# Expert stage: scatter products and transposes in two groups a slot, both conditional branches between the down products, no zero fill

## The chip, the cores and the metric

The kernel runs on one core of a Trainium2 chip. The metric is the device time of one execution in microseconds; of the kernel before there are three timed runs, and their median stands for it. All times below are in microseconds unless marked ns. TensorE's granted clock is either full (1.00, 2.4 GHz) or half (0.50, 1.2 GHz).

## The reference

Two network blocks over 512 tokens of width 1024, in float32. The change lies in the feed-forward part of the first block, a mixture of 32 experts in four groups; each token goes to the best two experts of its best group:

```python
g_sel = top_k(softmax(ht @ router_group), 1)
top_vals, top_idx = top_k(expert logits of that group, 2)
top_w = softmax(top_vals) * p_group
for every expert e:
    act = silu(ht @ w_gate[e]) * (ht @ w_up[e]) * combine[:, e]      # 1024 -> 256
    y = y + act @ w_down[e]                                          # 256 -> 1024
```

The result is scaled by a gain and added to the residual stream. The rest (a mixer with two kinds of recurrent heads ahead of it, and two attention and convolution blocks behind it) is not touched.

## The kernel before

**Slots.** The stage (`moe`, called from `moe_block`) goes through 16 slots. A slot serves two experts, x and x + 16, whose tokens share one tile of 128 rows: normally 64 rows each, and up to 32 more for one of the two where the other has few. The rows of a slot are gathered by an indirect DMA on POOL's queue into one of three buffers (`gather`, tile xg), scaled on ScalarE, and transposed on TensorE (`moe_xt`: tile pxt in PSUM, then xt by VectorE).

**Steps of a slot.** `moe_up` multiplies the transposed rows with gate and up weights (tile gu). Each expert uses only its half of the array's columns: one matmul for 64 columns into pgA, one for the other 64 into pgB, eight steps k of the contraction; two such products run side by side. A float32 product stands in the trace as two records, so one k is two pairs of records. If one of the two experts has more than 64 rows, a conditional branch adds products on 32 columns (`narrow`); else a zero fill writes those rows of the banks. `moe_act` is the activation step: ScalarE takes Silu of the gate half into tile sa or sb, VectorE multiplies by the token weight and the up half; there are four pieces, two for sa, two for sb. `moe_st` transposes sa and sb (tile pst, copied to st). `moe_down` multiplies with the down weights (tile dn) into two banks py, again on half columns, with a second conditional branch in the middle (`narrow` rows). ScalarE copies py to yh, rounded, and VectorE makes the rest yl. `moe_hot` makes a one-hot matrix toh of token numbers on VectorE. `moe_back` multiplies yh and yl with toh on the full array (tile pb), eight scatter groups of two products, and VectorE adds each into the residual stream xT.

**Order.** Each engine does its instructions in the order in which the program writes them; there is no planner in this stage. Slots overlap by that order: in iteration x the products of slot x run over k = 0 to 7; behind k = 1 come the transposes pst of slot x - 1; behind k = 1 to 6 one scatter group each of slot x - 2, and two behind k = 7. Then come the conditional products of slot x, its activation step, the transposes pxt and the gather for slot x + 1, the scaling for x + 2, and the down products of slot x - 1. In iterations 0 and 1 the routing of overflow tokens is done in between (`route_extra`, `route_extra2`). `pump` issues the weight loads on SP's queue at the end of an iteration, into rings of six gu and eight dn tiles.

**PSUM.** Tag c has four banks in rotation for pxt, pst, pb and py. Three banks of tag d and one of tag a hold pgA and pgB of two slots.

**Helpers.** All matmuls are recorded at L199 (`mm`), transposes at L202 (`tr`), ScalarE's work at L196, VectorE's at L205, L210, L214.

Of the kernel before, what the change touches and what calls it, by code (L numbers as in the profile page):

```python
# [10 lines left out]
F32 = mybir.dt.float32  # L11
# [10 lines left out]
P = 128  # L22
T = 512
D = 1024
KD = 8
# [150 lines left out]
class Build:  # L176
# [1686 lines left out]
        self.nc.vector.tensor_copy(st[:, 0:2 * n], pt[:, 0:2 * n * P].rearrange("p (k t) -> p k t", t=P))  # L1863
        return st

    def moe_down(self, mp, st, dn, wide, narrow=(), need=None):


        pys = [self.pc("py") for _ in dn]

        def part(k, parts, start, stop):
            for py, d in zip(pys, dn):
                for i, r, n in parts:
                    self.mm(py[r:r + n], st[:, 2 * i + k, r:r + n], d[i][:, k, :], start, stop)
        part(0, wide, True, False)
        if narrow:
            with self.tc.If(need > 0):
                for k in range(2):
                    part(k, narrow, False, False)
        part(1, wide, False, True)  # L1880
        ys = []
        for py in pys:
            yh, yl = [mp.tile([P, T], F32R, tag="y", bufs=4, name=n) for n in ("yh", "yl")]
            self.act(yh, py, AF.Copy)
            self.tt(yl, py, yh.bitcast(F32), OP.subtract)
            ys.append((yh, yl))
        return ys
# [67 lines left out]
    def moe(self, mp, pump, tab_d):  # L1955

        tab, ids = self.tab, self.ids
        n = NMAIN
        rows = ((slice(0, 64), slice(64, 96)), (slice(32, 64), slice(64, 128))), ((slice(0, 32), slice(64, 128)), (slice(0, 64), slice(96, 128)))

        parts = ((((0, 0, 64), (1, 64, 64)), ((0, 64, 32), (1, 32, 32))), (((1, 0, 64), (0, 64, 64)), ((0, 0, 32), (1, 96, 32))))
        g, xt, ps, s, st, y, oh, need = {}, {}, {}, {}, {}, {}, {}, {}

        def scale(x):
            if x < n:
                self.act(g[x], g[x], AF.Copy, scale=tab[:, 3, x:x + 1])

        def start(x):
            if x == 0:
                scale(x)  # L1970
            xt[x] = self.moe_xt(mp, g.pop(x))
            if x + 3 < n:
                g[x + 3] = self.gather(ids[:, x + 3:x + 4], x + 3)
            need[x] = self.nc.tensor.value_load(self.need[0:1, x:x + 1])
            ps[x] = [self.pd("pgA"), self.pd("pgB") if x % 2 == 0 else self.ps.tile([P, T], F32, tag="a", bufs=self.ps_a, name="pgB")]

        def narrow(x):

            with self.tc.If(need[x] > 0) as c:
                for k in range(KD):  # L1980
                    self.moe_up(ps[x], xt[x], gus, k, parts[x % 2][1])
            with c.Else():
                for i, r, m in parts[x % 2][1]:
                    self.mm(ps[x][i][r:r + m, :], self.zero[:, 0:m], self.zero)

        for x in range(3):
            g[x] = self.gather(ids[:, x:x + 1], x)
        pump(0, 0, eng="gpsimd")
        start(0)
        scale(1)  # L1990
        for x in range(n + 2):
            gus = [self.gus[x + 16 * i] for i in range(2)] if x < n else None
            for k in range(KD):
                if x < n:
                    self.moe_up(ps[x], xt[x], gus, k, parts[x % 2][0])
                if k == 1 and 0 < x <= n:
                    st[x - 1] = self.moe_st(mp, s.pop(x - 1))
                for j in ((), range(k - 1, k), range(6, KD))[min(k, 1) + k // 7] if x > 1 else ():
                    self.moe_back(y[x - 2][j // 4], oh[x - 2], j // 4, (j % 4,))
            if x < n:  # L2000
                narrow(x)
                i = x % 2
                s[x] = self.sA[i], self.sB[i]
                for e in range(2):
                    for r in rows[i][e]:
                        self.moe_act(s[x][e], ps[x][e], tab[:, 1 + e, x:x + 1], r)
                del ps[x], xt[x]
            if x + 1 < n:
                start(x + 1)
            if x + 2 < n:  # L2010
                scale(x + 2)
            if x == 0:
                self.route_extra([mp.tile([P, T], F32, tag="y", bufs=4, name="xs") for _ in range(4)])
            if x == 1:
                self.route_extra2()
                self.dma("scalar", tab_d, tab)
            if 0 < x <= n:
                c = x - 1
                y[c] = self.moe_down(mp, st.pop(c), [[self.dns[c + 16 * e, h] for e in range(2)] for h in range(2)],
                                     *parts[c % 2], need[c])  # L2020
                oh[c] = self.moe_hot(tab[:, 0, c:c + 1])
            pump(2 * (x + 1), 4 * x)

    def moe_extra(self, mp, mw, wg, wu, wd, tab_d, gu_bufs, dn_bufs):
# [763 lines left out]
```

## Time and profile before

| | |
|---|---|
| median of 3 runs | 2766.24 (2765.49 to 2769.7) |
| profiled execution | 2763.61, its span 2761.9 |
| TensorE busy | 2524.8 (91%) |
| VectorE busy | 1546.4 (56%) |
| ScalarE busy | 936.0 (34%) |
| POOL busy | 961.5 (35%) |
| mean DMA rate | 152 GB/s |

How to read it: a row of a timeline has the start, the duration, engine and line, the operation, output and inputs, and in square brackets the time for which the engine stood idle before it and who released it. Matmul records overlap, as the engine is pipelined: the distance between starts tells the rate, and the duration of one record is longer. The expert slots lie between 793 and 1133.

### The profile page before, as it was taken

The page shows a single profiled execution, that of the slowest core. Times are in us where ns is not written, and L with a number is a line of the kernel's source. Part 1 is how long each engine was busy: PE and PEld are TensorE (multiplying, and loading weights), DVE is VectorE, ACT ScalarE, POOL GpSimd, SP SyncE. Part 2 cuts the span into 40 slices and gives each one's busy share as a digit, 9 for nine tenths or more (in the row PEclk, how much of TensorE's full clock was granted, in tenths as well). Part 3 has the DMA queues.
Part 4 walks back from the last instruction along what each step waited for, and adds up shares of the span by engine and source line. Part 5 has one row for each costly group of instructions (what it writes and reads, how often), then busy time and mean ns, then how long its engine had stood idle before and what let it go on. Part 6 is the DMA issues. An engine that isn't in the chain of part 4 may idle for free.

```text
span 2761.9 us, 35101 instructions
## 1 busy us (share of the span) xinstructions
PE 2524.8 (91%) x13640; PEld 1839.8 (67%) x13640; DVE 1546.4 (56%) x2483; ACT 936.0 (34%) x1536; POOL 961.5 (35%) x649
## 2 busy tenths in 40 slices
PE   7777888787969999889999999999999999999999
PEld 4576776565633333556777777878766777888887
DVE  4996595454255655555455388885444345453523
ACT  3424223443221111233344332323332344442422
POOL 1444454422320000243563333434332343344443
PEclk8889998779979999899999999999999999999999
DMA  9356565643289984333455345553231325132321
GB/s 265 99 159 183 157 181 179 194 128 126 95 318 349 344 311 174 107 107 103 139 165 169 107 140 171 193 171 116 74 109 51 95 75 193 62 106 92 107 89 64
DMA packets 336316, 419.06 MB, mean 152 GB/s; under 512 B 37752, under 2 KB 279904, under 8 KB 327824
## 3 DMA queue, kind: packets, MB, share of 16 engines
q1 hardware_dynamic: 317008, 378.13, 42.1%
q10 hardware_dynamic: 14480, 24.23, 2.6%
q0 software_dynamic: 4656, 14.35, 1.6%
q8 instruction: 114, 1.87, 0.3%
q14 instruction: 58, 0.48, 0.1%
HBM read 387.64 MB, written 33.21 MB: 152 GB/s over the span
## 4 chain that ended last, share of the span: by engine, by line
PE 44%; DVE 6%; issue 3%; POOL 2%; ACT 2%; DMA 2%; ACTq 0%; POOLq 0%; DVEq 0%
PE pd L199 35%; DVE adacc L214 2%; PE psc L199 2%; POOL wlo L205 2%; PE tm L199 2%; PE ptot L199 1%; DMA raw<-in_w_up 1%; DVE cv L214 1%; PE pc L199 1%; PE po L199 1%; DVE h L214 1%; PE pz L199 1%; PE pso L199 1%; PE pst L199 1%; PE prr L199 1%
## 5 line engine op out<-in xcount | busy, mean ns | idle before, releaser
L205 POOL TENSOR_TENSOR wlo<-raw,whi 128x1024 fp32r<-128x1024 f32 (+3 forms) x317 | 721.6, 2283 | 1219.2 <-ACT whi L196 1068.1
L199 PE MATMUL pd<-h,whi 128*128 128x512 f32 (+1 forms) x3440 | 1096.0, 401 | 31.7 <-DVE stg L214 6.7
L199 PEld LDWEIGHTS pd<-h,whi 128*128 128x128 f32 x3440 | 646.3, 193 | 188.3 <-issue 28.6
L199 PE MATMUL pd<-h,wlo 128*128 128x512 f32 (+1 forms) x1720 | 673.8, 392 | 21.2 <-POOL wlo L205 21.2
L196 ACT ACTIVATE whi<-raw 128x1024 fp32r<-128x1024 f32 (+3 forms) x319 | 314.0, 994 | 264.4 <-PE pd L199 127.5
L199 PEld LDWEIGHTS pd<-h,wlo 128*128 128x128 f32 x1720 | 330.9, 192 | 93.5 <-POOL wlo L205 25.5
L214 DVE SCALAR_TENSOR_TENSOR adacc<-raw,cs,adacc 128x256 f32<-128x256 f32 x288 | 211.0, 733 | 9.4
L199 PE MATMUL pd<-fyh,whi 128*128 128x512 f32 (+1 forms) x546 | 205.4, 376 | 8.6 <-ACT whi L196 5.2
L214 DVE SCALAR_TENSOR_TENSOR cv<-pd,vec,cv 128x511 f32<-128x511 f32 (+1 forms) x176 | 131.8, 749 | 143.4 <-ACT cv L196 137.9
L199 PE MATMUL pd<-fyh,wlo 128*128 128x512 f32 (+1 forms) x546 | 202.0, 370 | 5.0 <-POOL wlo L205 5.0
L199 PE MATMUL pd<-fyl,whi 128*128 128x512 f32 (+1 forms) x546 | 202.1, 370 | 2.8 <-DVE fyl L205 2.8
L199 PE MATMUL pgB<-gu,xt 128*64 128x512 f32 (+1 forms) x304 | 153.7, 613 | 3.0 <-DVE xt L205 3.0
L199 PE MATMUL pgA<-gu,xt 128*64 128x512 f32 (+1 forms) x304 | 153.7, 613 | 0.0
L214 DVE SCALAR_TENSOR_TENSOR xTl<-pd,mod,xTl 128x512 f32<-128x512 f32 (+1 forms) x73 | 49.4, 683 | 186.1 <-PE pd L199 186.1
L199 PE MATMUL tm<-whi,h 128*128 128x256 f32 x640 | 129.3, 295 | 8.3 <-ACT whi L196 8.0
L214 DVE SCALAR_TENSOR_TENSOR xT<-pb,mod,xT 128x512 f32<-128x512 f32 x128 | 93.6, 748 | 77.2 <-PE pb L199 77.1
L199 PEld LDWEIGHTS pd<-fyh,whi 128*128 128x128 f32 x546 | 105.1, 192 | 39.8 <-ACT whi L196 8.9
L199 PEld LDWEIGHTS pd<-fyh,wlo 128*128 128x128 f32 x546 | 104.9, 192 | 24.3 <-POOL wlo L205 7.3
L199 PEld LDWEIGHTS pd<-fyl,whi 128*128 128x128 f32 x546 | 105.1, 192 | 19.6 <-DVE fyl L205 3.6
L199 PEld LDWEIGHTS tm<-whi,h 128*128 128x128 f32 x640 | 106.2, 199 | 9.6 <-ACT whi L196 8.3
L199 PE MATMUL tm<-wlo,h 128*128 128x256 f32 x320 | 93.3, 292 | 7.7 <-POOL wlo L205 7.6
L196 ACT ACTIVATE cv<-pd,vec 128x512 f32<-128x512 f32 x88 | 68.2, 776 | 94.6 <-PE pd L199 94.0
(563 smaller groups left out, 3404.5 us busy)
## 6 DMA issues: line engine op xcount, KB each, us to landing
raw<-in_ada SPq DMA_DIRECT2D x64, 1024.0 KB, 5.6
raw<-in_w_in SPq DMA_DIRECT2D x54, 1024.0 KB, 5.4
raw<-in_w_up SPq DMA_DIRECT2D x44, 1024.0 KB, 5.0
gu<-in_wg SPq DMA_DIRECT2D x30, 1024.0 KB, 4.8
gu<-in_wu SPq DMA_DIRECT2D x30, 1024.0 KB
dn<-in_wd SPq DMA_DIRECT2D x59, 512.0 KB, 4.7
raw<-in_w_dn SPq DMA_DIRECT2D x16, 1024.0 KB, 5.2
raw<-in_wo SPq DMA_DIRECT2D x12, 1024.0 KB, 5.2
```

The source lines that it names most:

```text
L196: return self.nc.scalar.activation(out, in_, func, **kw)
L199: return self.nc.tensor.matmul(out, lhsT, rhs, start=start, stop=stop)
L205: return (eng or self.nc.vector).tensor_tensor(out, a, b, op=op)
L214: return (eng or self.nc.vector).scalar_tensor_tensor(out, a, s, b, op0=op0, op1=op1)
```

## The change

`narrow` keeps only its taken branch; the zero fill of the rows that a slot doesn't use is done once for each of the two pairs of banks ahead of the first slot, and the banks are held in a list `banks` and not allocated anew. The transposes of the gathered rows, the gather, the load of the branch flag (`rows_of`) and the scaling move from the end of the iteration to k = 4 of the products before. The eight scatter groups come in fours behind k = 1 and k = 4. `moe_down` gets an argument `between`, and calls the conditional up products of the current slot between its first and second half; the activation step comes behind `moe_down` and `moe_hot`.

```diff
-    def moe_down(self, mp, st, dn, wide, narrow=(), need=None):
+    def moe_down(self, mp, st, dn, wide, narrow=(), need=None, between=None):
...
         part(0, wide, True, False)
+        if between is not None:
+            between()
         if narrow:
...
-        def start(x):
-            if x == 0:
-                scale(x)
+        def rows_of(x):
             xt[x] = self.moe_xt(mp, g.pop(x))
             if x + 3 < n:
                 g[x + 3] = self.gather(ids[:, x + 3:x + 4], x + 3)
             need[x] = self.nc.tensor.value_load(self.need[0:1, x:x + 1])
-            ps[x] = [self.pd("pgA"), self.pd("pgB") if x % 2 == 0 else self.ps.tile([P, T], F32, tag="a", bufs=self.ps_a, name="pgB")]
 
         def narrow(x):
 
-            with self.tc.If(need[x] > 0) as c:
+            with self.tc.If(need[x] > 0):
                 for k in range(KD):
                     self.moe_up(ps[x], xt[x], gus, k, parts[x % 2][1])
-            with c.Else():
-                for i, r, m in parts[x % 2][1]:
-                    self.mm(ps[x][i][r:r + m, :], self.zero[:, 0:m], self.zero)
...
-        start(0)
+
+        banks = [[self.pd("pgA"), self.pd("pgB")], [self.pd("pgA"), self.ps.tile([P, T], F32, tag="a", bufs=self.ps_a, name="pgB")]]
+        for x in range(2):
+            for i, r, m in parts[x][1]:
+                self.mm(banks[x][i][r:r + m, :], self.zero[:, 0:m], self.zero)
+        scale(0)
+        rows_of(0)
         scale(1)
         for x in range(n + 2):
             gus = [self.gus[x + 16 * i] for i in range(2)] if x < n else None
+            if x < n:
+                ps[x] = banks[x % 2]
+
             for k in range(KD):
                 if x < n:
                     self.moe_up(ps[x], xt[x], gus, k, parts[x % 2][0])
                 if k == 1 and 0 < x <= n:
                     st[x - 1] = self.moe_st(mp, s.pop(x - 1))
-                for j in ((), range(k - 1, k), range(6, KD))[min(k, 1) + k // 7] if x > 1 else ():
-                    self.moe_back(y[x - 2][j // 4], oh[x - 2], j // 4, (j % 4,))
+                if k == 4 and x + 1 < n:
+                    rows_of(x + 1)
+                    scale(x + 2)
+                    if x == 1:
+                        self.route_extra2()
+                        self.dma("scalar", tab_d, tab)
+                if k in (1, 4) and x > 1:
+                    self.moe_back(y[x - 2][k // 4], oh[x - 2], k // 4, range(4))
+            if 0 < x <= n:
+                c = x - 1
+                y[c] = self.moe_down(mp, st.pop(c), [[self.dns[c + 16 * e, h] for e in range(2)] for h in range(2)],
+                                     *parts[c % 2], need[c], (lambda: narrow(x)) if x < n else None)
+                oh[c] = self.moe_hot(tab[:, 0, c:c + 1])
+            elif x == 0:
+                narrow(0)
             if x < n:
-                narrow(x)
                 i = x % 2
                 s[x] = self.sA[i], self.sB[i]
                 for e in range(2):
                     for r in rows[i][e]:
                         self.moe_act(s[x][e], ps[x][e], tab[:, 1 + e, x:x + 1], r)
                 del ps[x], xt[x]
-            if x + 1 < n:
-                start(x + 1)
-            if x + 2 < n:
-                scale(x + 2)
             if x == 0:
                 self.route_extra([mp.tile([P, T], F32, tag="y", bufs=4, name="xs") for _ in range(4)])
-            if x == 1:
-                self.route_extra2()
-                self.dma("scalar", tab_d, tab)
-            if 0 < x <= n:
-                c = x - 1
-                y[c] = self.moe_down(mp, st.pop(c), [[self.dns[c + 16 * e, h] for e in range(2)] for h in range(2)],
-                                     *parts[c % 2], need[c])
-                oh[c] = self.moe_hot(tab[:, 0, c:c + 1])
             pump(2 * (x + 1), 4 * x)
```

On VectorE, from the transposed rows of one slot to the copy of pst, the order before was as follows (sa and sb are the tiles of the activation step, yl and toh belong to the down products of the slot before).

```order
L214 SCALAR_TENSOR_TENSOR sa_6321<-sa_6321,tab,pgA 32x256
L214 SCALAR_TENSOR_TENSOR sa_6321<-sa_6321,tab,pgA 64x256
L214 SCALAR_TENSOR_TENSOR sb_6323<-sb_6323,tab,pgB 64x256
L1877 UNCONDITIONAL_BRANCH
L214 SCALAR_TENSOR_TENSOR sb_6323<-sb_6323,tab,pgB 32x256
L205 TENSOR_TENSOR xt<-pxt,b_5891 128x512 x2
L205 TENSOR_TENSOR yl<-py,yh 128x512 x2
L210 TENSOR_SCALAR toh<-tokens,tab 128x512
L1863 COPY st<-pst 128x512
```

After the change the same stretch of VectorE stands so:

```order
L205 TENSOR_TENSOR xt<-pxt,b_5891 128x512 x2
L214 SCALAR_TENSOR_TENSOR xT<-pb,mod_81,xT 128x512 x4
L1978 UNCONDITIONAL_BRANCH
L1879 UNCONDITIONAL_BRANCH
L205 TENSOR_TENSOR yl<-py,yh 128x512 x2
L210 TENSOR_SCALAR toh<-tokens,tab 128x512
L214 SCALAR_TENSOR_TENSOR sa_6321<-sa_6321,tab,pgA 32x256
L214 SCALAR_TENSOR_TENSOR sa_6321<-sa_6321,tab,pgA 64x256
L214 SCALAR_TENSOR_TENSOR sb_6323<-sb_6323,tab,pgB 64x256
L214 SCALAR_TENSOR_TENSOR sb_6323<-sb_6323,tab,pgB 32x256
L1863 COPY st<-pst 128x512
```

The four products of the activation step have moved from ahead of xt and yl to behind yl and toh, directly ahead of the copy of pst.

On ScalarE the end of one iteration before:

```order
L1979 UNCONDITIONAL_BRANCH
L196 ACTIVATE sa_6321<-pgA 32x256
L196 ACTIVATE sa_6321<-pgA 64x256
L196 ACTIVATE sb_6323<-pgB 64x256
L196 ACTIVATE sb_6323<-pgB 32x256
L1877 UNCONDITIONAL_BRANCH
L196 ACTIVATE xg_6315<-xg_6315,tab 128x1024
L196 ACTIVATE yh<-py 128x512 x2
```

And after the change:

```order
L196 ACTIVATE xg_6315<-xg_6315,tab 128x1024
L1978 UNCONDITIONAL_BRANCH
L1879 UNCONDITIONAL_BRANCH
L196 ACTIVATE yh<-py 128x512 x2
L196 ACTIVATE sa_6321<-pgA 32x256
L196 ACTIVATE sa_6321<-pgA 64x256
L196 ACTIVATE sb_6323<-pgB 64x256
L196 ACTIVATE sb_6323<-pgB 32x256
```

The two copies yh, which read the down products, stood behind the four Silus and stand ahead of them now; the scaling of xg has moved to the front.

On TensorE the stretch around the gathered rows' transposes pxt, before:

```order
L199 MATMUL pgB<-zero 32x512
L1979 UNCONDITIONAL_BRANCH
L202 MATMUL pxt<-const_ident,xg_6315 128x128 x8
L1974 TENSOR_LOAD need
L199 MATMUL py<-dn,st 64x512 x4
```

And after:

```order
L199 MATMUL pgA<-gu,xt 64x512
L202 MATMUL pxt<-const_ident,xg_6315 128x128 x8
L1974 TENSOR_LOAD need
L199 MATMUL pb<-toh,yh 128x512
L199 MATMUL pb<-toh,yl 128x512
```

The zero fill ahead of pxt is gone, and pxt is followed by scatter products and not by the down products py.

## Rows read from the trace of the kernel before

**Rows 1.** Part 1 of the page: busy time, share of the span, instructions.

```profile
PE 2524.8 (91%) x13640; PEld 1839.8 (67%) x13640; DVE 1546.4 (56%) x2483; ACT 936.0 (34%) x1536; POOL 961.5 (35%) x649
```

**Rows 2.** Stretches: length, busy time of each engine, granted clock, DMA share, GB/s.

```profile
804.80:808.10 3.30, 2.69 (x7) 0.98 (x8) 2.98 (x6) 0.49 (x1) 0.65 (x1) 0.50 0.99 395
808.20:1128.90 320.70, 313.27 (x1338) 114.87 (x1335) 176.81 (x283) 56.53 (x105) 11.04 (x12) 1.00 0.74 275
1129.00:1132.30 3.30, 3.30 (x10) 2.52 (x9) 3.14 (x6) 0.00 (x0) 0.00 (x0) 0.50 0.00 0
861.40:880.10 18.70, 18.51 (x80) 7.02 (x78) 11.40 (x18) 3.72 (x8) 0.99 (x1) 1.00 0.94 348
```

**Rows 3.** TensorE's timeline, one slot: start, duration, operation.

```profile
842.66 0.59 PE L199 MATMUL pgB<-gu,xt 128*64 128x512 f32 x1
...
844.50 0.50 PE L202 MATMUL pst<-const_ident,sa 128*128 128x128 f32 x2
844.84 0.40 PE L202 MATMUL pst<-const_ident,sb 128*128 128x128 f32 x2
...
846.65 0.50 PE L199 MATMUL pb<-toh,yh 128*128 128x512 f32 x1
...
848.33 0.50 PE L199 MATMUL pb<-toh,yh 128*128 128x512 f32 x1
...
855.58 0.40 PE L199 MATMUL pb<-toh,yh 128*128 128x512 f32 x1
855.81 0.40 PE L199 MATMUL pb<-toh,yl 128*128 128x512 f32 x1
...
856.46 1.16 PE L202 MATMUL pxt<-const_ident,xg 128*128 128x128 f32 x8
857.55 1.94 PE L199 MATMUL py<-dn,st 128*64 128x512 f32 x8
859.67 1.94 PE L199 MATMUL py<-dn,st 128*64 128x512 f32 x8 [0.19 <-PEq L1877]
861.41 0.59 PE L199 MATMUL pgA<-gu,xt 128*64 128x512 f32 x1
```

**Rows 4.** ScalarE's timeline at the end of that slot.

```profile
856.56 0.37 ACT L196 ACTIVATE sa<-pgA 32x256 f32<-32x256 f32 x1 [13.01 <-PE pgB L199]
857.60 0.38 ACT L196 ACTIVATE sa<-pgA 64x256 f32<-64x256 f32 x1 [0.66 <-DVE sa L214]
```

**Rows 5.** VectorE's timeline, start and end of that slot.

```profile
844.20 0.48 DVE L210 TENSOR_SCALAR toh<-tokens,tab 128x512 fp32r<-128x512 f32 x1
845.28 0.69 DVE L1863 COPY st<-pst 128x512 f32<-128x512 f32 x1 [0.61 <-PE pst L202]
845.89 0.74 DVE L214 SCALAR_TENSOR_TENSOR xT<-pb,mod,xT 128x512 f32<-128x512 f32 x1
...
857.10 0.46 DVE L214 SCALAR_TENSOR_TENSOR sa<-sa,tab,pgA 32x256 f32<-32x256 f32 x1
858.01 0.49 DVE L214 SCALAR_TENSOR_TENSOR sa<-sa,tab,pgA 64x256 f32<-64x256 f32 x1 [0.45 <-ACT sa L196]
...
859.45 0.49 DVE L214 SCALAR_TENSOR_TENSOR sb<-sb,tab,pgB 32x256 f32<-32x256 f32 x1 [0.44 <-ACT sb L196]
```

**Rows 6.** TensorE's timeline, two waits in the first slots.

```profile
805.41 1.11 PE L199 MATMUL pgB<-gu,xt 128*64 128x512 f32 x1 [2.96 <-DVE xt L205]
...
826.26 0.47 PE L199 MATMUL pb<-toh,yh 128*128 128x512 f32 x1 [1.60 <-DVE toh L210]
```

**Rows 7.** ScalarE's timeline, iteration 1's end.

```profile
822.63 1.15 ACT L196 ACTIVATE xg<-xg,tab 128x1024 f32<-128x1024 f32 x1 [4.87 <-DMA xg<-xa_d,ids]
...
823.80 1.08 ACT L196 ACTIVATE yh<-py 128x512 fp32r<-128x512 f32 x2
```

**Rows 8.** TensorE's timeline, two waits after the last slot.

```profile
1114.19 0.47 PE L199 MATMUL pb<-toh,yh 128*128 128x512 f32 x1 [1.28 <-DVE toh L210]
...
1127.64 0.47 PE L199 MATMUL pb<-toh,yh 128*128 128x512 f32 x1 [1.91 <-DVE toh L210]
```

## Prediction

> **What bounds the kernel now.** I read the page first: TensorE is busy for 91% of the span, more than any other engine [rows 1]. Then the table of stretches. From 808.2 to 1128.9, which is nearly all of the expert slots, TensorE is busy for 313.27 of 320.70 us at a granted clock of 1.00, VectorE for 176.81, ScalarE for 56.53; in one ordinary slot the DMA engines are busy 0.94 of the time [rows 2]. So TensorE sets the pace there and the others have slack. The questions are what the change takes off TensorE and whether something now makes it wait.
>
> The TensorE timeline of one slot shows where its time goes [rows 3]. A slot begins with its first half-column product, at 842.66; the next begins at 861.41: 18.75. TensorE comes to pst, the transposes of the previous slot's activations, 1.84 after the slot's start. Half-column products run in pairs: the four pairs of the down products from 859.67 to 861.41 take 0.43 each. Scatter products (pb) that stand together start 0.235 apart (855.58, 855.81). But from one lone scatter group to the next, 846.65 to 848.33, it is 1.68, and that stretch holds two scatter products and two pairs: 2 x 0.235 + 2 x 0.43 = 1.33. The missing 0.34 is the price of going from half columns to the full array and back.
>
> Last I read ScalarE and VectorE at the slot's end [rows 4, 5]. The activation step (sa and sb: ScalarE's Silu, then VectorE's product, in four pieces) starts right behind the slot's own products, at 856.56, and its last product ends at 859.45 + 0.49 = 859.94. The transposes that need it come 1.84 after 861.41, at 863.25. It has 3.3 us in hand.
>
> **What the change removes.** Before, a slot leaves half columns eight times: for pst at k = 1, for the lone scatter groups at k = 2 to 6, for the two groups at k = 7, and for pxt, which the zero fill cuts off from them. After the change it does so twice: for pst with four scatter groups at k = 1, and for pxt with four at k = 4. Without the zero fill pxt would follow the last scatter product by 0.235, at 856.05 and not at 856.46 [rows 3]: 0.41. Five more round trips at 0.34 are 1.70. Together 2.11 a slot.
>
> **What it adds on TensorE.** Both skipped branches now stand between the halves of the down products. One skip there shows as 857.55 to 859.67 = 2.12 for four pairs that take 1.72, so 0.40 [rows 3]. The second costs nothing if the sequencer is ahead and 0.40 if it isn't; I take 0.3, since the first, with as much work queued before it, wasn't hidden. Net saving 1.8, which makes a slot of 16.95 if nothing waits. The two zero fills that remain, ahead of the first slot, lie in TensorE's wait for the first gathered rows; without that cover they would cost under 1 us, once.
>
> **What it moves, and the new wait.** On ScalarE and VectorE the activation step now stands behind the results of the down products: ScalarE does yh twice and then the Silus, VectorE yl twice, toh, and then the four products. yh needs the down products, the last thing in the slot. Counted from the next slot's start (842.66), toh starts at 844.20 and ends at +2.02 [rows 5]. The first activation product cannot start earlier. From the start of the first (857.10) to the end of the last (859.94) is 2.84, since the second Silu of a tile waits for the first product on it (0.66, [rows 4]) and the second product for that Silu (0.45, [rows 5]). So sb is ready at +4.8, when TensorE has stood at pst since +1.84. It uses 0.34 of that for the two transposes of sa (844.50 to 844.84, [rows 3]), which is ready at 2.02 + 1.40 = +3.4 (857.10 to 858.50, [rows 5]). It waits about 1.55 before them and 1.1 after them: 2.65 a slot. Behind pst stand the four scatter groups and the rest of the slot; nothing overtakes, as at 826.26, where TensorE stood 1.60 for toh with half-column products queued behind [rows 6]. Nothing hides this wait, since it follows the slot's end at a fixed distance.
>
> Scatter groups in fours need four banks of PSUM. VectorE frees one in 0.74 [rows 5]; the fourth group takes the bank of pst, whose copy (0.69, [rows 5]) ends before TensorE has issued three groups (6 x 0.235 = 1.41). No cost. The transposes pxt and their load of the branch flag move to k = 4, and with them the gather on POOL's queue and the scaling of gathered rows on ScalarE. They come half a slot earlier; the weight loads on SP's queue keep their place at the slot's end. No cost in an ordinary slot: the scaling ends long before yh. If a gather were late there, yh would be, as at the start.
>
> **Start and end.** Moving pxt of slot 1 into slot 0 removes a wait of 2.96, at 805.41 [rows 6]. But the scaling of a later slot's rows waits for their gather until 822.63, and yh follows at 823.80 [rows 7]. That scaling still stands ahead of the first yh, so toh ends where it did, just ahead of the first scatter product at 826.26 [rows 6], and now the activation step follows it, 2.84, and the transposes of sb. The scatter starts 2.9 later, and what the start gained is lost. At the end likewise: TensorE waited 1.28 for toh, until 1114.19 [rows 8], and now the step comes behind toh: 2.9.
>
> **The clock.** The wait of 2.96 was followed by half clock (1.2 GHz) from 804.8 to 808.1, one of 1.91 by half clock from 1129.0 to 1132.3; those of 1.60 and 1.28 were not, the clock being 1.00 from 808.2 to 1128.9 [rows 2, 6, 8]. At half clock products take twice as long, so a stretch of 3.3 loses 1.6. The new wait adds up to the size of those that cost the clock, but comes in two pieces of the size of those that did not. Bounds: 0 and 1.6 a slot. I take half of 13 slots, and the longer waits at the start and the end: 8.5 x 1.6 = 13.6. The Trainium skill ("TensorE: Matmul & The Clock Gate", section "Why this matters for your kernels") warns only of longer idle gaps between bursts than these; by it the clock would hold and the sum below be 13.6 lower. The trace speaks against it, since the wait of 1.91 did cost the clock.
>
> **Sum.** Saving in slots 2 to 15: 14 x -1.8 = -25.2. Wait in slots 3 to 15: 13 x 2.65 = +34.5. Start +2.9, end +2.9, clock +13.6. Together +28.7 on a profiled execution of 2763.6 (its span is 2761.9): 2792. The median of the three runs, 2766.2, is 2.6 above that execution, so I forecast 2794 for it.
>
> **Rivals.**
> 1. The same wait, but the clock holds in all slots (the pieces are as short as 1.60 and 1.28): 28.7 - 13.6 = +15.1, 2781. Chance 0.14. This is the case that the Trainium skill's page named above would have.
> 2. The same wait, and the clock falls in every slot: 15 x 1.6 = 24 in place of 13.6, +39.1, 2805; with the second skip at its full 0.40, 2807. Chance 0.18.
> 3. Faster: no wait, because the activation step gets done beside the down products. It decides at 1.8, below which a wait leaves each slot a gain. For it: VectorE and ScalarE are idle for half of the stage [rows 2], and the step's input is ready before the second half of the down products. Against it: both would have to do the step ahead of yh and yl, and their queues have it behind. It would give 14 x -1.8 = -25, 2741. There the DMA engines would begin to bind: 0.94 of 18.75 = 17.6 a slot, so 1.15 and not 1.8 in the nine slots without second branches, 2747. Chance 0.12.
> 4. The two cancel: a wait of about 2 at full clock, or more saved on the switches: within 0.2%. Chance 0.08.
>
> My forecast has 0.48. Slower by over 0.2% (5.5 us, about what a measurement of this kernel can tell from no change) are the forecast and rivals 1 and 2: 0.80. Same 0.08, faster 0.12. The range leaves out rival 3 and part of rival 4 and adds little beyond rival 2: 2770 to 2808.
>
> **What would show it.** In the changed profile pst should have a wait of some 1.5 in front of sa, released by VectorE's sa, and some 1.1 in front of sb. Lone scatter groups should be gone, with products 0.235 apart in fours. Ordinary slots should last 19.6, or 21.2 where the clock fell, and the granted clock of the stage be below 1.00. I am wrong if the idle time before and within pst is under 1.8 a slot, or if a slot without it takes more than 17.3.

## The result and the profile after

| | before | changed |
|---|---|---|
| median of 6 runs, us | 2767.97 (2763.85 to 2770.92) | 2780.04 (2774.91 to 2786.41) |
| profiled execution, us | 2763.6 | 2784.94 |
| its span, us | 2761.9 | 2783.2 |

The change makes the kernel slower: the ratio is 1.0058, with a 95% interval of 1.004 to 1.0076; by the medians it is some 12 us, by the ratio some 16. The page of the changed kernel, part 1, answers to [rows 1]:

```profile
PE 2503.2 (90%) x13618; PEld 1854.3 (67%) x13618; DVE 1539.5 (55%) x2483; ACT 933.9 (34%) x1536; POOL 960.4 (35%) x649
```

TensorE is busy for 21.6 us less than before, and the span is 21.3 longer. So the change did take work off TensorE, and time in which TensorE does nothing took its place. The table of stretches shows where (length, busy time of each engine, granted clock, DMA share, GB/s; answers to [rows 2]):

```profile
844.40:1139.80 295.40, 255.06 (x1110) 113.99 (x1106) 145.18 (x237) 47.84 (x94) 8.91 (x9) 0.95 0.69 259
848.90:852.30 3.40, 3.10 (x9) 2.52 (x10) 2.33 (x4) 0.90 (x1) 0.00 (x0) 0.50 1.02 346
865.40:885.00 19.60, 16.59 (x78) 7.67 (x76) 10.94 (x18) 3.66 (x8) 0.99 (x1) 1.00 0.89 333
```

The first line holds slots 3 to 15: TensorE is idle for 40 of 295 us, where it was idle for 7 of 321 before, and the mean clock is 0.95 and no longer 1.00. The second is a piece of slot 3 at half clock. The third is slot 4, one of those that stayed at full clock: 19.67 long and not 18.75. TensorE's timeline of slot 4 answers to [rows 3]; the slot goes from its first half-column product, at 865.38, to that of the next, at 885.05:

```profile
865.38 0.59 PE L199 MATMUL pgA<-gu,xt 128*64 128x512 f32 x1
...
868.77 0.50 PE L202 MATMUL pst<-const_ident,sa 128*128 128x128 f32 x2 [1.47 <-DVE sa L214]
870.20 0.51 PE L202 MATMUL pst<-const_ident,sb 128*128 128x128 f32 x2 [0.94 <-DVE sb L214]
...
871.02 0.39 PE L199 MATMUL pb<-toh,yh 128*128 128x512 f32 x1
871.25 0.39 PE L199 MATMUL pb<-toh,yl 128*128 128x512 f32 x1
...
875.24 1.16 PE L202 MATMUL pxt<-const_ident,xg 128*128 128x128 f32 x8
...
880.82 1.89 PE L199 MATMUL py<-dn,st 128*64 128x512 f32 x8
883.31 1.94 PE L199 MATMUL py<-dn,st 128*64 128x512 f32 x8 [0.60 <-PEq L1879]
885.05 0.59 PE L199 MATMUL pgB<-gu,xt 128*64 128x512 f32 x1
```

Both new waits stand at pst, one in front of sa and one in front of sb, each released by VectorE's product. pst starts 3.39 after the slot's start, where it was 1.84 [rows 3], and its sb pair follows the sa pair by 1.43, where it was 0.34. By starts the wait is 1.55 + 1.09, together 2.64. The idle column shows less, 1.47 + 0.94 = 2.41, since the profile models the ends of matmuls. The scatter products now come in fours, 0.23 apart, and the lone groups are gone.

VectorE's timeline behind the end of slot 4, at 885.05, shows what TensorE waits for in slot 5 (answers to [rows 5]):

```profile
886.59 0.48 DVE L210 TENSOR_SCALAR toh<-tokens,tab 128x512 fp32r<-128x512 f32 x1
886.98 0.47 DVE L214 SCALAR_TENSOR_TENSOR sa<-sa,tab,pgA 64x256 f32<-64x256 f32 x1
...
889.32 0.49 DVE L214 SCALAR_TENSOR_TENSOR sb<-sb,tab,pgB 64x256 f32<-64x256 f32 x1 [0.45 <-ACT sb L196]
```

toh ends 2.02 after the start of slot 5, the four activation products come behind it, and the last ends at 889.81, 4.76 after it: the chain that the prediction wrote down (2.02, then 2.84, +4.8). At the stage's start TensorE's timeline answers to [rows 6] and ScalarE's to [rows 7]:

```profile
826.46 0.67 PE L202 MATMUL pst<-const_ident,sa 128*128 128x128 f32 x2 [6.57 <-DVE sa L214]
...
828.16 0.77 PE L199 MATMUL pb<-toh,yh 128*128 128x512 f32 x1
```

```profile
821.52 1.15 ACT L196 ACTIVATE xg<-xg,tab 128x1024 f32<-128x1024 f32 x1 [16.96 <-DMA xg<-xa_d,ids]
```

The scaling of gathered rows still waits for its gather, until 821.52 (822.63 before [rows 7]), and yh, toh and now the activation step stand behind it; TensorE waits 6.57 for sa. The stage began at 792.44, and the first scatter product comes 35.72 later; before it was 826.26 - 793.41 = 32.85 [rows 6]. Toward the end of this wait, and of a wait of 3.18 that follows the last slot, the clock falls to half; the third row is the rest of the stage:

```profile
825.00:831.80 6.80, 4.66 (x12) 3.12 (x12) 4.71 (x9) 2.28 (x4) 0.00 (x0) 0.50 1.04 423
1139.00:1145.80 6.80, 5.21 (x14) 3.95 (x15) 4.75 (x8) 1.02 (x3) 0.00 (x0) 0.50 0.00 0
1145.90:1160.70 14.80, 12.83 (x55) 5.54 (x54) 7.94 (x13) 1.19 (x2) 0.00 (x0) 1.00 0.01 2
```

For the account by stretches I took TensorE's first products of slots 0, 3 and 15 and the last scatter product, of before:

```profile
793.41 1.12 PE L199 MATMUL pgA<-gu,xt 128*64 128x512 f32 x1
...
1087.70 0.59 PE L199 MATMUL pgB<-gu,xt 128*64 128x512 f32 x1
...
1132.77 0.40 PE L199 MATMUL pb<-toh,yl 128*128 128x512 f32 x1
```

and of the changed kernel, with the wait at pst behind the last slot and the last wait for toh:

```profile
792.44 1.12 PE L199 MATMUL pgA<-gu,xt 128*64 128x512 f32 x1
...
844.39 0.59 PE L199 MATMUL pgB<-gu,xt 128*64 128x512 f32 x1
...
1111.17 0.59 PE L199 MATMUL pgB<-gu,xt 128*64 128x512 f32 x1
...
1139.85 0.70 PE L202 MATMUL pst<-const_ident,sa 128*128 128x128 f32 x2 [3.18 <-DVE sa L214]
...
1156.80 0.47 PE L199 MATMUL pb<-toh,yh 128*128 128x512 f32 x1 [1.97 <-DVE toh L210]
...
1160.66 0.39 PE L199 MATMUL pb<-toh,yl 128*128 128x512 f32 x1
```

| stretch | before | after | moved by | the prediction's terms |
|---|---|---|---|---|
| ahead of the first expert product | 793.41 | 792.44 | -0.97 | 0 |
| slots 0 to 2 | 49.25 | 51.95 | +2.70 | 2.9 - 1.8 + 1.6 = +2.7 |
| slots 3 to 14 | 245.04 | 266.78 | +21.74 | 12 x 0.85 + 6 x 1.6 = +19.8 |
| slot 15 and the last scatter | 45.07 | 49.49 | +4.42 | 0.85 + 0.8 + 2.9 + 1.6 = +6.15 |
| behind the last scatter product | 1629.13 | 1622.54 | -6.6 | 0 |

Inside the stage the sum came out at +28.9, against +28.7 forecast. That it is so close is in part luck: slots 3 to 14 cost 1.9 more than forecast, slot 15 and the end 1.7 less. The rest gave 7.6 back, in code that the change does not touch: the stretch behind the stage ran at a mean clock of 0.98 before and of 0.99 after, and its 7218 matmuls took 8.7 us less:

```profile
1132.80:2761.90 1629.10, 1561.64 (x7218) 1226.68 (x7216) 881.08 (x1303) 592.33 (x940) 648.17 (x392) 0.98 0.37 119
```

```profile
1160.70:2783.20 1622.50, 1552.90 (x7218) 1219.33 (x7216) 878.92 (x1305) 591.95 (x940) 646.99 (x392) 0.99 0.37 119
```

### The profile page after: what moved, and what is told of

It is laid out like the page before. It is cut to its first block, busy times and chain, and to the rows that moved or that the text cites. A ratio compares the mean times of both kernels' runs of the same rounds, so it can differ in the third digit from the quotient of the medians.

```text
span 2783.2 us, 35058 instructions
## 1 busy us (share of the span) xinstructions
PE 2503.2 (90%) x13618; PEld 1854.3 (67%) x13618; DVE 1539.5 (55%) x2483; ACT 933.9 (34%) x1536; POOL 960.4 (35%) x649
## 3 DMA queue, kind: packets, MB, share of 16 engines
q8 instruction: 113, 1.85, 0.3%
## 4 chain that ended last, share of the span: by engine, by line
PE 43%; DVE 7%; issue 3%; ACT 2%; POOL 2%; DMA 2%; ACTq 0%; POOLq 0%; DVEq 0%
PE pd L199 34%; DVE adacc L214 2%; PE psc L199 2%; POOL wlo L205 2%; PE tm L199 2%; PE ptot L199 1%; DMA raw<-in_w_up 1%; DVE h L214 1%; DVE cv L214 1%; PE po L199 1%; PE pz L199 1%; PE pso L199 1%; PE pc L199 1%; PE pst L199 1%; PE prr L199 1%
## 5 line engine op out<-in xcount | busy, mean ns | idle before, releaser
L199 PE MATMUL pd<-h,wlo 128*128 128x512 f32 (+1 forms) x1720 | 673.3, 391 | 21.2 <-POOL wlo L205 21.2
L199 PE MATMUL pgB<-gu,xt 128*64 128x512 f32 (+1 forms) x304 | 141.2, 601 | 0.3 <-PEq L1978 0.3
L199 PE MATMUL pgA<-gu,xt 128*64 128x512 f32 (+1 forms) x304 | 141.2, 601 | 0.0
L196 ACT ACTIVATE yh<-py 128x512 fp32r<-128x512 f32 x32 | 19.0, 597 | 249.6 <-PE py L199 249.5
```

What stands on the lines that cost most here:

```text
L196: return self.nc.scalar.activation(out, in_, func, **kw)
L199: return self.nc.tensor.matmul(out, lhsT, rhs, start=start, stop=stop)
```

## The experiments

The theory: each slot saves about 1.7 to 1.8 of TensorE's time, and loses more, since the activation step now stands behind the results of the down products; the pieces of the wait then cost the clock in part of the slots. The rivals said that the scatter in fours or the skipped branches eat the saving, that DMA engines begin to bind, or that the slots at half clock are an accident. Times of different series are compared only by their ratio to before, which ran beside them (2767.82 beside the first four, 2761.24 beside the next four).

**The groups of four alone** (before, with one edit):

```diff
-                for j in ((), range(k - 1, k), range(6, KD))[min(k, 1) + k // 7] if x > 1 else ():
-                    self.moe_back(y[x - 2][j // 4], oh[x - 2], j // 4, (j % 4,))
+                if k in (1, 4) and x > 1:
+                    self.moe_back(y[x - 2][k // 4], oh[x - 2], k // 4, range(4))
```

> The kernel before with one edit: the eight scatter groups come in fours behind k = 1 and k = 4, and not one by one. Theory (each excursion to the full array costs 0.34 us; five fewer a slot): ordinary slots 18.75 - 1.70 = 17.05 us, the whole 14 x 1.70 = 24 us less, 2744 us. Rival (groups of four wait for banks of PSUM that VectorE frees at 0.74 us each, and give the saving back): slots of 18 us or more, 2757 us or more.

Measured: 2738.36 us, ratio 0.9895 [0.9877, 0.9914]. TensorE's timeline of a slot, 895.64 to 912.82 = 17.18:

```profile
895.64 0.59 PE L199 MATMUL pgA<-gu,xt 128*64 128x512 f32 x1
...
907.54 0.39 PE L199 MATMUL pgB<-zero 128*32 128x512 bf16 x1
...
912.82 0.59 PE L199 MATMUL pgB<-gu,xt 128*64 128x512 f32 x1
```

The zero fill is still there, ahead of pxt. The grouping alone saves 18.75 - 17.18 = 1.57 a slot, in which five round trips between half columns and the full array go: 0.31 each, where the prediction read 0.34. TensorE's products wait for no bank. The stage is 23.2 shorter (339.4 to 316.2), near the 24 expected; the rest of the gain, by which the time is under the expected 2744, lies outside it. The Trainium skill ("TensorEngine Tiling (Array Packing)", section "Key Properties") says that a change of tiling mode drains TensorE; that a round trip has a price agrees with it, and 0.31 is the price here.

**The zero fill alone** (before, with the banks filled once ahead of the first slot):

```diff
...
-            with self.tc.If(need[x] > 0) as c:
+            with self.tc.If(need[x] > 0):
...
-            with c.Else():
-                for i, r, m in parts[x % 2][1]:
-                    self.mm(ps[x][i][r:r + m, :], self.zero[:, 0:m], self.zero)
...
```

> The kernel before without the zero fill in the slots; the banks are filled once ahead of the first slot. Theory (pxt follows the last scatter product directly): 0.41 us less in slots whose branch is skipped, 18.34 us an ordinary slot, the whole 4 to 6 us less than before, about the uncertainty. Rival (skipping past the branch costs as much as the fill did): slots stay at 18.75 us.

Measured: 2754.4, ratio 0.9981 [0.9962, 0.9999]; slots of 18.62, so 0.13 saved and not the expected 0.41. TensorE's timeline at that place:

```profile
889.31 0.40 PE L199 MATMUL pb<-toh,yl 128*128 128x512 f32 x1
889.86 0.35 PE L202 MATMUL pxt<-const_ident,xg 128*128 128x128 f32 x1
```

pxt comes 0.55 behind the last scatter product, where it was 0.65 [rows 3] and was to be 0.235. So 0.10 of the 0.41 goes and 0.31 stays, with no product in it. The skipped branch is all that the program has for TensorE at this place: I put the 0.31 to it, and take it that the fill had hidden it. No run shows the place without a branch.

**The same kernel with the old order of the activation step** (the changed kernel; `narrow` and the step stand ahead of the down products again, as before; the scaling of rows goes back to the end of the iteration):

```diff
                 if k == 4 and x + 1 < n:
                     rows_of(x + 1)
-                    scale(x + 2)
...
-            if 0 < x <= n:
...
-            elif x == 0:
-                narrow(0)
             if x < n:
+                narrow(x)
                 i = x % 2
                 s[x] = self.sA[i], self.sB[i]
...
+            if 0 < x <= n:
+                c = x - 1
+                y[c] = self.moe_down(mp, st.pop(c), [[self.dns[c + 16 * e, h] for e in range(2)] for h in range(2)],
+                                     *parts[c % 2], need[c])
+                oh[c] = self.moe_hot(tab[:, 0, c:c + 1])
+            scale(x + 2)
```

> The changed kernel with its fours, pxt at k = 4 and no zero fill, but with the conditional up products and the activation step right behind the slot's products again, ahead of the down products, and the scaling of rows back at the end of the iteration. Theory (all that the change saves stays, the wait at pst and the late yh at the start go): ordinary slots 16.9 us, no wait at pst, clock 1.00 in slots 3 to 15, the whole 2726 to 2737 us, under all kernels so far. Rival (the saving is bounded by the weight loads, which take 0.94 of 18.75 us): slots of 17.6 us, 2740 us or more.

Measured: 2729.14, ratio 0.9887 [0.9869, 0.9904]; faster than both kernels. By the ratio it can't be told from the groups of four alone, but its stage is the shortest, 308.8 against 316.2. TensorE's timeline of a slot, 872.83 to 889.85 = 17.02, and the stretch of slots 3 to 15:

```profile
872.83 0.59 PE L199 MATMUL pgB<-gu,xt 128*64 128x512 f32 x1
...
874.68 0.50 PE L202 MATMUL pst<-const_ident,sa 128*128 128x128 f32 x2
...
889.85 0.59 PE L199 MATMUL pgA<-gu,xt 128*64 128x512 f32 x1
```

```profile
838.80:1085.80 247.00, 242.09 (x1110) 104.19 (x1106) 141.04 (x233) 47.57 (x91) 8.91 (x9) 1.00 0.82 312
```

18.75 - 1.57 - 0.13 = 17.05, so the two savings add up. pst starts 1.85 after the slot's start and waits for nothing, and the clock is 1.00. The DMA engines do not make TensorE wait: a slot of 17.0 is below the 17.6 of rival 3. But they have nothing in hand either: over slots 3 to 9 (838.80 to 957.90) their share is 1.01, and only later slots bring it down to the 0.82 of the stretch. What more such slots in a row would do isn't shown. This is the change without its loss, so the loss lies in what went back: the places of the conditional products, of the activation step and of the scaling. The next experiment moves the step alone.

**The activation step ahead of the results** (the changed kernel, with the step taken from behind the down products and written at the end of `narrow`, between their halves):

```diff
         def narrow(x):
...
+            i = x % 2
+            s[x] = self.sA[i], self.sB[i]
+            for e in range(2):
+                for r in rows[i][e]:
+                    self.moe_act(s[x][e], ps[x][e], tab[:, 1 + e, x:x + 1], r)
...
```

> The changed kernel with the activation step written right behind the conditional up products, between the halves of the down products, so that ScalarE does the four Silus and VectorE the four products ahead of yh, yl and toh. Nothing else differs. Theory (the step's place behind the down products makes TensorE wait 2.4 us a slot at pst, and the wait costs the clock): the waits of 1.46 and 0.93 us at pst go, the granted clock is 1.00 in the slots, ordinary slots last 17.3 us plus at most 0.7 us for banks that yl and the copy of pst free later, and the whole is 2745 to 2758 us, under the kernel before. Rival (the second branch between the down products and the scatter groups in fours cost what the change lost): the slots stay at 19.7 and 21.2 us and the whole at 2775 to 2785 us.

Measured: 2745.21, ratio 0.9922 [0.9907, 0.9937]. TensorE's timeline of a slot and the stretch:

```profile
876.14 0.59 PE L199 MATMUL pgB<-gu,xt 128*64 128x512 f32 x1
...
877.99 0.51 PE L202 MATMUL pst<-const_ident,sa 128*128 128x128 f32 x2
...
879.17 0.47 PE L199 MATMUL pb<-toh,yh 128*128 128x512 f32 x1 [0.44 <-DVE toh L210]
...
893.75 0.59 PE L199 MATMUL pgA<-gu,xt 128*64 128x512 f32 x1
```

```profile
840.90:1094.60 253.70, 242.19 (x1111) 105.42 (x1107) 139.85 (x233) 45.28 (x89) 8.90 (x9) 1.00 0.80 301
```

The wait at pst is gone and the clock holds, with nothing moved but the step. The slot is 17.61, 0.6 above the one of the experiment before: now toh, which stands behind the step, is the late one, 0.44 in the idle column. One chain on VectorE and ScalarE feeds both pst and the scatter, and what stands last in it is late.

**pst later in the slot** (the changed kernel):

```diff
-                if k == 1 and 0 < x <= n:
+                if k == 4 and 0 < x <= n:
```

> The changed kernel with the transposes pst behind k = 4, ahead of pxt, and not behind k = 1. The orders of ScalarE's and VectorE's activation step, yh, yl and toh are those of the changed kernel. Theory (it is the distance from the slot's end to pst that is too short: the activations are ready 4.8 us after it, and pst would now come 6.6 us after it): no wait at pst, clock 1.00, ordinary slots 17.3 to 17.7 us, the whole 2743 to 2755 us. Rival (the waits come from ScalarE and VectorE being late for something else, or from the branches): slots of 19 us or more, 2770 us or more.

Measured: 2744.27 (2738.11 to 2751.79), ratio 0.9924 [0.9904, 0.9944]. Here the step keeps the change's order, and only the reader of its result moves:

```profile
872.38 0.59 PE L199 MATMUL pgB<-gu,xt 128*64 128x512 f32 x1
874.54 0.47 PE L199 MATMUL pb<-toh,yh 128*128 128x512 f32 x1 [0.25 <-DVE toh L210]
...
879.30 0.51 PE L202 MATMUL pst<-const_ident,sa 128*128 128x128 f32 x2
...
889.59 0.59 PE L199 MATMUL pgA<-gu,xt 128*64 128x512 f32 x1
```

At 6.92 after the slot's start, pst waits for nothing; the slot is 17.21, a little under the 17.3 to 17.7 expected. So it is the distance from the slot's end to pst that decides, as the prediction had it, and not the order by itself.

**Keeping TensorE at work during the first piece** (the changed kernel; six products of zeros go into pst's bank ahead of its transposes, which overwrite them):

```diff
         pt = self.pc("pst")
+        if n == 2:
+            for _ in range(6):
+                self.mm(pt, self.zero[:, 0:P], self.zero)
```

> The changed kernel with six filler products of zeros on the full array, 512 columns each, written into the bank of pst ahead of its transposes, which overwrite it. They take 1.4 us and stand where TensorE waits 1.46 us for sa. Theory (of what the change loses some 13 to 16 us are half clock that follows the wait): the wait before sa is filled, the one of 0.93 us before sb stays, the granted clock is 1.00 in the slots, all ordinary slots last 19.7 to 19.9 us and none 21.2, the whole is 2764 to 2770 us. Rival (the clock falls for another reason, or products of zeros don't count): half clock stays in half of the slots, 2778 to 2788 us.

Measured: 2771.74 (2768.01 to 2782.67), ratio 1.0023 [1.0007, 1.0039]. TensorE's timeline of a slot, one of the six records missing, and the stretch of slots 3 to 15:

```profile
880.78 1.47 PE L199 MATMUL pst<-zero 128*128 128x512 bf16 x5
882.31 0.50 PE L202 MATMUL pst<-const_ident,sa 128*128 128x128 f32 x2
883.75 0.51 PE L202 MATMUL pst<-const_ident,sb 128*128 128x128 f32 x2 [0.94 <-DVE sb L214]
```

```profile
839.50:1121.10 281.60, 261.61 (x1175) 112.89 (x1184) 141.02 (x232) 46.26 (x90) 8.90 (x9) 1.00 0.73 271
```

The filler saves no wait: pst starts as late as before and ordinary slots last 19.64 to 19.98. But in the profiled execution the clock stays at 1.00 in every one of slots 3 to 15, and the stage is 11.2 shorter than in the changed kernel (368.2 to 357.0), 10.6 of it in slots 3 to 14, of which eight had lost the clock. That is the price of the clock by itself: 1.3 in each of the eight. The median missed the expected time by little, on the high side, but the 12 runs fall into two groups: eight took 2768 to 2773, the profiled one (2769.38) among them, and four 2780 to 2783, the rival's times. Whether the filler failed to hold the clock in those four isn't shown.

**The two skipped branches apart** (the changed kernel, with `narrow(x)` ahead of the down products, so that one skip stands between their halves and one ahead of them):

```diff
+            if x < n:
+                narrow(x)
...
-                                     *parts[c % 2], need[c], (lambda: narrow(x)) if x < n else None)
+                                     *parts[c % 2], need[c])
...
```

> The changed kernel with the conditional up products ahead of the down products, so that one skip and not two stands between the halves; the activation step stays behind the down products. Theory (the second skip between the halves costs 0.37 us: 2.49 against 2.12 us from the first half's start to the second's): slots without half clock 19.3 us in place of 19.67, the waits at pst as in the changed kernel. Rival (a skip costs the same wherever it stands): 19.67 us.

Measured in one run: 2784.02. Slots at full clock last 19.74, where the theory had 19.3 and the rival 19.67.

```profile
921.89 1.94 PE L199 MATMUL py<-dn,st 128*64 128x512 f32 x8 [0.31 <-PEq L1978]
923.98 1.94 PE L199 MATMUL py<-dn,st 128*64 128x512 f32 x8 [0.15 <-PEq L1879]
```

Apart the skips idle TensorE for 0.31 and 0.15, together for 0.60. The halves stand 0.40 closer, but the slot isn't shorter: the theory missed, and putting the branches side by side neither gains nor loses what could be seen.

**Both kernels again.** Unchanged kernels, for the slots at half clock and for the parts of the span outside the stage:

> The changed kernel once more, for a second profile. Theory (which slots lose the clock depends on where the wait falls, and so differs from execution to execution, and so does the half clock behind the stage): the waits at pst are again 1.46 and 0.93 us in each slot; the number of slots with half clock is between 5 and 10 of 13, not the same slots as in the first profile; the stage lasts 362 to 373 us; the time is 2774 to 2788 us. Rival (the half clock is fixed by the program): the same slots, the same stage of 370 us.

> The kernel before, unchanged, for a second profile. The stage took 28.9 and 28.6 us more in the two profiles of the changed kernel, but the medians differ by 12 and 16 us. Theory (the difference lies outside the stage, where the code is the same and the half clock varies from execution to execution): the stage lasts 341 us again; what lies outside it is anywhere from 2408 to 2424 us, as in the profiles so far, not fixed at the 2420.6 us of the first profile. Rival (the changed stage itself makes what follows shorter): outside the stage again 2419 to 2424 us.

> The kernel before, unchanged, for a third profile; as for the second: the stage 341 us, outside it 2408 to 2424 us by the theory, 2419 to 2424 us by the rival.

> The changed kernel, for a third profile. The stage 368 to 371 us with half clock in the same eight slots as in the first two profiles; outside it 2408 to 2424 us by the theory that this part varies, 2408 to 2414 us by the rival that the changed stage shortens it.

Measured, one run each: the changed kernel 2780.13 and 2778.72, before 2772.51 and 2766.81. The first repeat of the changed kernel had half clock in the same slots as the profile above: 3, 5, 7, 8, 10, 11, 13 and 14. The second had it in 3, 5, 7, 9, 10, 12, 13 and 15. So about every second slot loses its clock, and which ones is not fixed, though the first repeat didn't show it and missed its expectation. The account of all six profiles, in us:

| | ahead of the stage | stage | behind it |
|---|---|---|---|
| before, three profiles | 793.4, 798.5, 795.7 | 339.4, 340.5, 340.4 | 1629.1, 1631.8, 1628.9 |
| changed, three profiles | 792.4, 791.1, 787.1 | 368.2, 367.9, 367.9 | 1622.5, 1619.3, 1622.0 |
| difference of the means | -5.7 | +27.9 | -8.7 |

The stage repeats to within 1.2 us. What lies outside it was shorter by 14.4 on the mean, and 27.9 - 14.4 = +13.5, between the 12 of the medians and the 16 of the ratio. For before the expectations missed. It took 2422.5 outside the stage in its first profile and then 2430.3 and 2424.6, more than either range; the changed kernel took 2415.0, 2410.5 and 2409.1. With three profiles each the two do not overlap, so it doesn't just vary from execution to execution. Nor can the rival be all of it, since the part ahead of the stage, which the stage can't shorten, was shorter too; over all kernels that part took 786.8 to 798.5. The stretch behind the stage took 1629 to 1632 for before, 1629.3 with the activation step first and 1629.2 with the old order; 1619 to 1626 for all the others, the fours alone and before without the fill among them (1623.0 and 1623.3). Its code is the same, and its time goes with its granted clock: by the traces' records of the granted clock it had 63 to 70 us of half clock in the three profiles of before and 41 to 48 in the three of the changed kernel. What sets this was not found; length of the stage does not (316.2 and 368.2 both have the shorter stretch).

## Why the prediction came out as it did

The forecast was 2794, slower; it was slower, 2780. The sign and the mechanism were right, and one assumption that the prediction never stated was wrong. Both of its own signs of being wrong stayed away: the waits at pst are 2.64 a slot, over 1.8, and a slot without them is 17.03, under 17.3.

- **The wait.** Forecast as 1.55 before sa and 1.1 before sb, 2.65 by starts; measured 1.55 and 1.09. The distances that carried it stood in the trace of before.
- **The saving.** Forecast 1.8 a slot; a slot without its wait is 19.67 - 2.64 = 17.03, so 1.72. The term mis-sized is the five round trips: 1.57 measured alone, not 1.70. The fill and the second skip nearly cancelled, as the sum had it, but not for its reasons: removing the fill saved 0.13 a slot and not 0.41, as 0.31 of that was most likely a skip under the fill, and the skip that was to be added between the halves was this same one, moved. Net 0.11 by the prediction, 1.72 - 1.57 = 0.15 measured.
- **An ordinary slot** was to last 19.6, or 21.2 with the clock lost. It lasted 19.67, or 20.88 to 21.21.
- **The clock.** Forecast was half of 13 slots at 1.6; it was 8 of 13 in each of three profiles, at 1.2 to 1.5. The experiment with the filler shows it as a cost of its own, 11.2 us. The Trainium skill's page on the clock gate, by which it would hold ("TensorE: Matmul & The Clock Gate", section "Why this matters for your kernels"), doesn't agree with these runs: none of the gaps in slots 3 to 15 is longer than 1.50.
- **Start and end.** The scatter's start came 35.72 - 32.85 = 2.87 later, forecast 2.9. From there to slot 3 it took 844.39 - 828.16 = 16.23, before 842.66 - 826.26 = 16.40 [rows 3, 6]: the half clock until 831.8 ate nearly all of the 1.7 that slot 2 saves, so by this estimate it cost about 1.5, forecast 1.6. Slot 15 and the end moved by 4.42 and not 6.15. Slot 15 kept its clock in this profile, for which the sum has 0.8. And I charged half clock to the end, though before already paid for one there, behind its wait of 1.91 [rows 2, 8]. The changed kernel pays earlier and for longer, from 1139.0 to 1145.8, but partly while TensorE waits, and pays nothing behind its last wait, of 1.97.
- **What failed** is the last step, "Together +28.7 on a profiled execution of 2763.6". It took what lies outside the stage to stay as it was. There the two kernels differ by 14 us on the mean of three profiles, about half of the stage's loss, and that is most of the 14 us between forecast and median. Nothing in the one profile of before showed that those parts vary.

Rival 1 (the clock holds, 2781) has nearly the measured time for another reason: its clock didn't hold; the 0.95 and the slots of 21 exclude it, and the filler shows what it would have given, a stage 11 shorter; that it meets the time is luck. Rival 2 (the clock falls in every slot) is excluded by the slots of 19.67. Rival 3 (no wait, 2741 to 2747) is excluded by the waits at pst; its gain came once the order of the step was undone, ratio 0.9887, and its brake, DMA at 17.6 a slot, did not act in the seven slots of 17.0. Rival 4 (within 0.2%) is excluded by the interval, from 0.4% up.

## What to carry to other kernels

Before a step is moved behind the last result of a stage, measure the distance from that result to the first reader of the step, and the length of the chain between: here 1.84 against 4.8 turned a gain of 1.7 a slot into a loss. Group work by the part of the array that it uses (0.31 a round trip here), but keep what the next slot reads first at the head of its engines' queues. A sum over one stage is good for that stage; how far the rest of the span moves by itself takes several profiles of the unchanged kernel, and of others, to see.

## What the hardware showed that I had not expected

- Two waits, of 1.47 and 0.94 in the idle column with two transposes between, were followed by 3.4 us of half clock in about every second slot. With the first filled by six products of zeros, the second of 0.94 alone cost none in 13 slots of the one profile; nor did a lone 0.44 or 0.25 in the two experiments above. Whether the first alone would have cost the clock isn't shown. Before, 1.60 and 1.28 had cost none and 1.91 did [rows 2, 6, 8].
- The length of a wait by itself doesn't settle it. The last wait for toh, 1.91, was followed by half clock in all three profiles of before. With the groups of four alone it was 1.91 too, and the clock stayed at 1.00 to the last scatter product; so it did in the changed kernel behind 1.97. In the groups of four alone:

```profile
1108.54 0.48 PE L199 MATMUL pb<-toh,yh 128*128 128x512 f32 x1 [1.91 <-DVE toh L210]
```

```profile
1108.50:1112.40 3.90, 3.86 (x15) 2.78 (x16) 3.12 (x5) 0.00 (x0) 0.00 (x0) 1.00 0.01 2
```

- Products of zeros in bf16 can hold the clock through a wait: 1.00 in that stretch of the filler's profile, against 0.95 without them.
- A conditional branch that is skipped left TensorE idle for 0.15 to 0.31 at its place, and for 0.60 where two stand in a row. Taking its else branch out gained 0.13 a slot, much less than the 0.41 that I read for it.
- Unchanged code behind the changed stage differed by up to 12 us between profiles of different kernels (1619.3 to 1631.8), longer where it had more half clock; the cause is open.
